# RWKV time mixing on one core: batch 1 in two blocks of 1024 tokens, and the output weight loaded as float32 by the sync queue

## The chip, the core and the metric

The kernel runs on one NeuronCore of a Trainium2 chip. The core has a matrix engine (TensorE, PE in the profile; PEld is its loading of stationary operands), a vector engine (VectorE, DVE), a scalar engine (ScalarE, ACT), a general engine (GpSimd, POOL) and a sync engine (SyncE, SP). Each of them works through its own instructions strictly in the order of the program, and they meet only at semaphores. Transfers are issued by SP, ACT or POOL and carried out by 16 DMA engines, which all queues share. In this kernel POOL issues the transfers that change float32 to bfloat16 on the way (queue q0 in the profile), and SP issues those that only copy (queue q1).

The metric is the device time of one execution, in microseconds (us); lower is better. About 1% (2 us) is what a measurement of this kernel can tell from no change.

## What is computed

```python
batch, seq_len, d_model = (16, 2048, 256)
x_prev[:, 1:, :] = x[:, :-1, :]                      # row 0 is zero
xv = x * time_mix_v + x_prev * (1 - time_mix_v)
xr = x * time_mix_r + x_prev * (1 - time_mix_r)
v = xv.reshape(-1, d_model) @ value_weight
r = xr.reshape(-1, d_model) @ receptance_weight
out = (1 / (1 + exp(-r)) * v) @ output_weight        # float32
```

The reference also computes a key product, which no output depends on.

## The kernel before

The 16 x 2048 tokens are worked in 64 units of 512 tokens (`TU`), four to a batch. For each unit TensorE transposes the tokens so that the 256 features lie on partitions (L272; from batch 10 on the DMA does it), multiplies by the receptance weight into `psum_r` and by the value weight into `psum_v` (both L384, four matmuls of 512 columns), and multiplies the product of the two by the output weight into `psum_o` (L416, eight matmuls of 256 columns, with `wo_bf` as the moving operand). VectorE makes the mixed inputs (scale L354, add L376) and the product `z_sb` of sigmoid and value (L697). ScalarE copies transposes out of PSUM (L289), makes the sigmoids (L658) and copies results out (L471). GpSimd does one half of some scalings (L364) and the small shift copies described next.

**Order on TensorE.** The loop over units `g` (L646) writes the order by hand: the receptance product of unit g, transposes of later units (`advance`, with `START_T = [1, 3, 5, 6, 7, 9, ...]`), the value product of unit g, then the output product of unit g-1. So the first use of `wo_bf` is the output product of unit 0, which stands at the end of loop step 1, behind the value product of unit 1 and ahead of the receptance product of unit 2. The transposes of units 4 and 5, the first two of batch 1, stand in step 2.

**Layout of the tokens.** A transposed unit lies in slots of 128 columns, one slot for each of the j-th tokens of all partitions. The previous token of slot j is slot j-1; the previous token of the first slot is the last slot, one column on. So each separately laid out stretch has one more slot in front, and `wrap_slots` fills it: a copy of 254 elements from the last slot (L557), and a copy of the first column from the stretch before (L554). Batches 0 and 1 (`BYUNIT = 2`) are laid out unit by unit: in DRAM order partition p of a unit holds tokens 4p to 4p+3, so four stretches a batch. Batches from 2 on have one stretch of 2048 tokens. A piece can be scaled only when the last slot of its stretch is transposed.

**Loads at the start.** SP issues units 0 and 1 of batch 0 as float32 (L174, in halves), the receptance weight (L180) and the value weight (L184). GpSimd waits until the receptance weight has landed, and then issues, with the cast to bfloat16: units 2 and 3 of batch 0 (L192), the output weight (L195), and batch 1 as four transfers of one unit (`load(1)`, L152). Batch 2 follows in loop step 1 (`load(2)`, L162), later batches at the places in `LOADS`.

**Stores.** Results of batches 0 and 1 are stored for two units at a time (L474), each partition's rows in two runs of 4 KB.

Of the kernel before, what the change touches and what calls it, by code (L numbers as in the profile page):

```python
# [8 lines left out]
FP32 = mybir.dt.float32  # L9
# [6 lines left out]
def kernel(  # L16
# [25 lines left out]
    nc = tc.nc  # L42

    B, S, D = x.shape
    P = 128
    KO = D // P
    J = S // P
    UJ = 4
    TU = UJ * P
    UB = J // UJ  # L50
    NU = B * UB
    LOOK = 6
    BYUNIT = 2
    LONG = 2
    H = UJ // 2
    STAGED = 10
# [40 lines left out]
    opool = ctx.enter_context(tc.tile_pool(name="opool", bufs=NO))  # L97
# [6 lines left out]
    SYNC = mybir.DependencyInfo(mybir.DependencyClass.Sync, mybir.DependencyReason.DATA)  # L104
# [5 lines left out]
    x_bf = {}  # L110
# [5 lines left out]
    o_sb = {}  # L116
# [12 lines left out]
    def unit_rows(t, b, e, n=1):  # L129

        return t[b, e * TU : (e + n) * TU, :].rearrange("(e p j) d -> p e j d", p=P, j=UJ)

    def new_staged(group):

        x_both[group[0]] = dpool.tile([len(group), PAD + S, D], BF16, name="x_natural")
        for k in range(len(group)):
            x_bf[group[0] + k] = x_both[group[0]][k, PAD:].rearrange("(p j) d -> p j d", p=P)
        return [(group[0], k) for k in range(len(group))]
# [8 lines left out]
    def load(b):  # L147
        if b < STAGED:
            x_bf[b] = xpool.tile([P, J, D], BF16, name="x_bf")
        if b < BYUNIT:  # L150
            for e in range(UB):
                nc.gpsimd.dma_start(  # L152
                    out=x_bf[b][:, e * UJ : (e + 1) * UJ, :], in_=unit_rows(x, b, e)[:, 0]
                )
            return
        if b in HALVED:
            return [
                nc.gpsimd.dma_start(out=x_bf[b][:, j : j + J // 2], in_=rows(b)[:, j : j + J // 2])
                for j in (0, J // 2)
            ]  # L160
        run = 8192 if b < LONG else 16384
        return nc.gpsimd.dma_start(out=x_bf[b], in_=rows(b), max_dma_last_dim=run)  # L162
# [4 lines left out]
    for m, tm in enumerate([time_mix_r, time_mix_v]):  # L167
        nc.scalar.dma_start(
            out=tm_rows[m * KO : (m + 1) * KO, :], in_=tm.rearrange("(ko p) -> ko p", p=P)
        )  # L170

    def load_halves(e):
# [8 lines left out]
        out=w_f32[:, 0], in_=receptance_weight.rearrange("(ko p) n -> p ko n", p=P)  # L181
# [6 lines left out]
    w_prev = consts.tile([P, KO, D], BF16)  # L188
    wo_bf = consts.tile([P, KO, D], BF16)
    x_first = xpool.tile([P, 2, UJ, D], BF16, name="x_bf")  # L190
    for e in (2, 3):
        op = nc.gpsimd.dma_start(out=x_first[:, e - 2], in_=unit_rows(x, 0, e)[:, 0])  # L192
        if e == 2:
            tc.add_manual_dep(op.ins, first_weight.ins.name, SYNC, reason="behind the weight")
    nc.gpsimd.dma_start(out=wo_bf, in_=output_weight.rearrange("(ko p) n -> p ko n", p=P))  # L195
    load(1)

    ones = nc.const_aps.tensor_like(1.0, zeros)
    wide = nc.const_aps.tensor_like(1.0, wo_bf.rearrange("p k d -> p (k d)"))
# [60 lines left out]
    def transposes(i):  # L260

        b, e = divmod(i, UB)
        if b > 0 and e == 0:
            new_xt(b)
        if b >= BYUNIT:
            e = (e - 1) % UB
        j0 = 1 + e * UJ + (e if b < BYUNIT else 0)
        if b < BYUNIT or e == UB - 1:
            late_copies.append((b, e))

        def one(ps, jj, ko, src, idn):
            nc.tensor.transpose(  # L272
                out=ps[:, jj], in_=src[:, jj, ko * P : (ko + 1) * P], identity=idn
            )

        if i == 1:
            for h in (1, 0):
                ps = ps_t_pool.tile([P, H, KO, P], FP32, name="ps_t")
                for jj in range(H):
                    for ko in range(KO):  # L280
                        one(ps[:, :, ko], jj, ko, x_unit[:, i, h * H : (h + 1) * H], ident_f)
                nc.scalar.copy(out=xt[b][:, j0 + h * H : j0 + (h + 1) * H], in_=ps)  # L282
            return
        ps = ps_t_pool.tile([P, UJ, KO, P], BF16, name="ps_t")
        src = x_first[:, e - 2] if b == 0 else x_bf[b][:, e * UJ : (e + 1) * UJ, :]
        for jj in range(UJ):
            for ko in range(KO):
                one(ps[:, :, ko], jj, ko, src, ident)
        nc.scalar.copy(out=xt[b][:, j0 : j0 + UJ], in_=ps)  # L289
        if i in SHIFT_ACT:  # L290
            j, n = (j0 - 1, UJ) if b < BYUNIT else (0, J)
            nc.scalar.copy(out=xt[b][:, j, :, 1:P], in_=xt[b][:, j + n, :, 0 : P - 1])
            shifted.append((b, e))

# [19 lines left out]
    def slots(piece, off=0):  # L314

        b, _, lo, hi = piece
        j = lo // P + (lo // TU if b < BYUNIT else 0) + off
        return slice(j, j + (hi - lo) // P)

    def by_unit(cols, lo, hi):  # L320
# [135 lines left out]
    def output(g, z):  # L456
        b, e = divmod(g, UB)
        if e % 2 == 0:
            new_o(b, e // 2)
        o = o_sb[b, e // 2]  # L460
        j0 = e % 2 * UJ
        if g >= NU - 4:
            for h in range(2):
                ps = ps_t_pool.tile([P, H, D], FP32, name="ps_t")
                out_matmuls(ps, z, b, h * H, H, whole=True)
                nc.scalar.copy(out=o[:, j0 + h * H : j0 + (h + 1) * H, :], in_=ps)
            store(nc.sync, b, e * UJ, (e + 1) * UJ)
            return
        ps = ps_o_pool.tile([P, UJ, D], FP32, name="psum_o")
        out_matmuls(ps, z, b, 0, UJ)  # L470
        nc.scalar.copy(out=o[:, j0 : j0 + UJ, :], in_=ps)  # L471
        if b < BYUNIT:
            if e % 2 == 1:
                nc.sync.dma_start(  # L474
                    out=unit_rows(out, b, e - 1, 2), in_=o.rearrange("p (e j) d -> p e j d", j=UJ)
                )
        elif g >= SINGLE:
            store(nc.sync, b, e * UJ, (e + 1) * UJ)
        elif e % 2 == 1:
            pair = (b, (e - 1) * UJ, (e + 1) * UJ)  # L480
            if g in FIRST:
                firsts.setdefault(FIRST[g], []).append(pair)
            elif g in WAITING:
                kept.setdefault(WAITING[g], []).append(pair)
            else:
                store(nc.sync, *pair)
# [46 lines left out]
    def pieces(g):  # L533

        b, e = divmod(g, UB)
        tile_for(g // 2)
        return [(b, m, e * TU, (e + 1) * TU) for m in range(2)]

    def wrap_slots(piece, one=None, after=None):


        b, _, lo, _ = piece
        by_unit = b < BYUNIT
        key = (b, lo // TU if by_unit else UB - 1)
        if key not in late_copies:
            return
        kos = slice(0, KO) if one is None else slice(one, one + 1)
        if one in (None, KO - 1):
            late_copies.remove(key)
        j = slots(piece).start if by_unit else 0  # L550
        n = UJ if by_unit else J
        if by_unit and j > 0:
            engine = nc.vector if key == (0, 1) else nc.gpsimd
            engine.tensor_copy(out=xt[b][:, j, kos, 0:1], in_=xt[b][:, j - 1, kos, P - 1 : P])  # L554
        if key in shifted:
            return
        op = (nc.vector if after is None else nc.gpsimd).tensor_copy(  # L557
            out=xt[b][:, j, kos, 1:P], in_=xt[b][:, j + n, kos, 0 : P - 1]
        )
        if after is not None:  # L560
            tc.add_manual_dep(op.ins, after.ins.name, SYNC, reason="one at a time")
# [15 lines left out]
    for ko in range(KO):  # L577
        nc.vector.tensor_scalar(
            out=w_prev[:, ko, :],
# [6 lines left out]
        out=w_bf[:, 0, 0, :], in0=w_f32[:, 0, 0, :], scalar1=tms[:, 0, 0:1], scalar2=None, op0=ALU.mult  # L586
    )
    nc.scalar.activation(
        out=w_bf[:, 0, 1, :], in_=w_f32[:, 0, 1, :], func=ACT.Copy, scale=tms[:, 0, 1:2]
# [3 lines left out]
    for ko in range(KO):  # L593
        nc.vector.tensor_scalar(
            out=w_bf[:, 1, ko, :],
# [39 lines left out]
    def scale_act(piece, kos):  # L635
        b, m, _, _ = piece
        for ko in kos:
            nc.scalar.activation(  # L638
                out=mixed(piece, ko),
                in_=tokens(piece, 0, ko),  # L640
                func=ACT.Copy,
                scale=c_sb[:, m, ko : ko + 1],
            )

    z_prev2 = z_prev = None
    for g in range(NU - 1):  # L646
        ps_r = ps_r_pool.tile([P, KO, TU], FP32, name="psum_r")
        if g == 0:
# [5 lines left out]
            last = add(pieces(1)[0])  # L654
# [16 lines left out]
                scale_act(p[0], (0,))  # L671
        for p in [q for q, _ in products[g]] + pooled[g]:
            last_unit_of = p[3] // TU - 1
            need = last_unit_of if p[0] < BYUNIT else min(last_unit_of + 1, UB - 1)
            assert UB * p[0] + need < tnext, (g, p, tnext)
            if g > AHEAD or p not in pooled[g]:
                wrap_slots(p)
        if g == 1:
            load(2)
            scale_act(pieces(2)[1], (1,))  # L680
        for p, kos in products[g]:
            if not (g - 1 >= FREE and p[1] == 1):
# [66 lines left out]
```

## Time and profile before

| | us |
|---|---|
| Time, median of 3 runs | 199.61 |
| The three runs | 199.41, 199.61, 200.61 |
| Span of the profiled execution, first to last instruction | 197.1 |
| Median less span | 2.5 |
| TensorE busy | 191.5 |
| VectorE busy | 183.1 |
| ScalarE busy | 177.1 |
| GpSimd busy | 86.3 |

The profile is one execution; its device time isn't listed by itself beside its span, so the 2.5 us between the span and the median stand here for what lies around the instructions. Times inside the trace count from the first instruction. In the timeline view a row gives the start, the length from the first to the last of the merged instructions, engine, line and operation, and in square brackets the idle time of that engine just before it with what ended it. In the view of the DMAs, a row of an issue gives the size at the destination and the time from the issue to the landing; a row of a queue gives the packets, the bytes at the destination, and the time that its packets took, as a share of 16 engines over the window asked for.

### The profile page before, as it was taken

Reading aid. Unit: us, or ns where it says so; the run is one execution under the profiler, and the core shown is the slowest. Engines: PE = TensorE matmul, PEld = TensorE weight load, DVE = VectorE, ACT = ScalarE, POOL = GpSimd, SP = SyncE. Lnnn points to the kernel's source line nnn. Section 1 sums busy time; section 2 is a strip of 40 time slices with the busy share of each in tenths; the row PEclk is TensorE's granted clock in tenths of the full one; section 3 lists DMA queues with packets and bytes.
Section 4 is the critical chain, followed back from the end, with each engine's and each line's share of the span. In section 5 each row is a group of like instructions: output and inputs, shape, how many; then the busy total and the mean of one; then the engine's idle time right before and its main releaser. Section 6 shows DMA issues by size and latency. Waiting matters only on the chain.

```text
span 197.1 us, 3735 instructions
## 1 busy us (share of the span) xinstructions
PE 191.5 (97%) x1358; PEld 123.0 (62%) x1364; DVE 183.1 (93%) x286; ACT 177.1 (90%) x197; POOL 86.3 (44%) x117
## 2 busy tenths in 40 slices
PE   8999999999999999999999999999999999999992
PEld 3556676666666666666666666666666666666660
DVE  0999999999999999999999999999999999999962
ACT  3699899999999999999999999999999999999982
POOL 2845542443665635624334266444433444444200
PEclk9999999999999999999999999999999999999998
DMA  5999999999999999999999999999999999999985
GB/s 185 238 176 224 218 254 262 247 259 262 296 413 283 283 296 332 283 238 198 376 209 290 335 346 186 212 218 241 290 290 419 419 421 419 416 416 421 382 327 221
DMA packets 35593, 58.13 MB, mean 295 GB/s; under 512 B 26004, under 2 KB 27128, under 8 KB 30840
## 3 DMA queue, kind: packets, MB, share of 16 engines
q1 hardware_dynamic: 31792, 41.34, 60.3%
q0 software_dynamic: 3632, 16.44, 41.6%
q8 instruction: 10, 0.16, 0.3%
q10 hardware_dynamic: 152, 0.13, 0.2%
q14 instruction: 7, 0.06, 0.1%
HBM read 34.34 MB, written 39.90 MB: 377 GB/s over the span
## 4 chain that ended last, share of the span: by engine, by line
PE 90%; DMA 6%; POOL 1%; issue 0%; SPq 0%; ACT 0%
PE psum_r L384 27%; PE psum_v L384 27%; PE psum_o L416 27%; PE ps_t L272 8%; DMA x_bf<-in_x_dram 4%; DMA w_f<-n_receptance_weight_dram 2%; PE ps_t L416 1%; POOL x_bf L192 1%; SPq L174 0%; POOL wo_bf L195 0%; PE psum_v L416 0%; POOL x_bf L152 0%; PE ps_t L384 0%; PE psum_r L416 0%; ACT x_bf L446 0%
## 5 line engine op out<-in xcount | busy, mean ns | idle before, releaser
L364 POOL TENSOR_SCALAR mix<-xt_both,c_sb 128x1024 bf16<-128x1024 bf16 (+1 forms) x55 | 61.1, 1110 | 85.5 <-DVE mix L376 82.3
L697 DVE TENSOR_TENSOR z_sb<-s_sb,psum_v 128x1024 bf16<-128x1024 bf16 (+1 forms) x64 | 76.8, 1201 | 2.3 <-PE psum_v L384 1.1
L376 DVE TENSOR_TENSOR mix<-mix,xt_both 128x1024 bf16<-128x1024 bf16 x112 | 76.8, 696 | 1.4
L384 PEld LDWEIGHTS <-w_bf 128*128 128x128 bf16 x512 | 48.5, 98 | 39.2 <-DVE mix L376 0.8
L658 ACT ACTIVATE s_sb<-psum_r 128x1024 bf16<-128x1024 f32 x63 | 65.2, 1034 | 6.2 <-PE psum_r L384 6.0
L384 PE MATMUL psum_v<-mix,w_bf 128*128 128x512 bf16 (+1 forms) x252 | 64.8, 378 | 0.4 <-DVE mix L376 0.2
L384 PE MATMUL psum_r<-mix,w_bf 128*128 128x512 bf16 x250 | 64.6, 379 | 0.2
L416 PE MATMUL psum_o<-wo_bf,z_sb 128*128 128x256 bf16 x486 | 63.2, 273 | 0.0
L416 PEld LDWEIGHTS <-z_sb 128*128 128x128 bf16 x512 | 52.0, 103 | 17.9 <-DVE z_sb L510 0.7
L471 ACT COPY o_sb<-psum_o 128x1024 f32<-128x1024 f32 x50 | 51.2, 1023 | 5.0 <-PE psum_o L416 4.8
L289 ACT COPY xt_both<-ps_t 128x1024 bf16<-128x1024 bf16 x32 | 32.9, 1039 | 0.0
L272 PEld LDWEIGHTS <-x_bf 128*128 128x128 bf16 x304 | 19.8, 98 | 8.4 <-DMA x_bf<-in_x_dram 0.4
L272 PE MATMUL ps_t<-ident,x_bf 128*128 128x128 bf16 x304 | 22.7, 219 | 0.2 <-DMA x_bf<-in_x_dram 0.2
L354 DVE TENSOR_SCALAR mix<-xt_both,c_sb 128x1024 bf16<-128x1024 bf16 (+1 forms) x47 | 21.3, 463 | 0.0
L638 ACT ACTIVATE mix<-xt_both,c_sb 128x1024 bf16<-128x1024 bf16 x14 | 16.3, 1163 | 0.0
L376 DVE TENSOR_TENSOR mix<-mix,xt_first 128x1024 bf16<-128x1024 bf16 x15 | 10.5, 708 | 0.1
L471 ACT COPY x_bf<-psum_o 128x1024 f32<-128x1024 f32 x10 | 10.2, 1015 | 0.0
L354 DVE TENSOR_SCALAR mix<-xt_first,c_sb 128x512 bf16<-128x512 bf16 x22 | 6.6, 350 | 0.3 <-ACT xt_first L282 0.2
L289 ACT COPY xt_first<-ps_t 128x1024 bf16<-128x1024 bf16 x6 | 6.0, 1022 | 0.0
L557 POOL COPY xt_first<-xt_first 128x254 bf16<-128x254 bf16 x5 | 2.0, 392 | 7.2 <-DVE mix L376 7.2
L162 POOL DMA_DIRECT2D x_bf<-in_x_dram x8 | 4.7, 584 | 0.0
L364 POOL TENSOR_SCALAR mix<-xt_first,c_sb 128x512 bf16<-128x512 bf16 x6 | 4.1, 685 | 1.3 <-DVE mix L376 0.8
(68 smaller groups left out, 52.3 us busy)
## 6 DMA issues: line engine op xcount, KB each, us to landing
out_dram<-o_sb SPq DMA_DIRECT2D x25, 1024.0 KB, 12.1
x_bf<-in_x_dram POOLq DMA_DIRECT2D x8, 1024.0 KB, 15.8
x_natural<-in_x_dram POOLq DMA_DIRECT2D x4, 1024.0 KB, 11.8
out_dram<-x_bf SPq DMA_DIRECT2D x4, 1024.0 KB, 14.4
x_natural<-in_x_dram POOLq DMA_DIRECT2D x4, 512.0 KB, 12.7
out_dram<-x_bf SPq DMA_DIRECT2D x4, 512.0 KB, 4.7
x_bf<-in_x_dram POOLq DMA_DIRECT2D x6, 256.0 KB, 7.0
o_sb<-in_x_dram SPq DMA_DIRECT2D x4, 256.0 KB, 3.9
```

The lines of the kernel that those rows point to most:

```text
L162: return nc.gpsimd.dma_start(out=x_bf[b], in_=rows(b), max_dma_last_dim=run)
L272: nc.tensor.transpose(out=ps[:, jj], in_=src[:, jj, ko * P : (ko + 1) * P], identity=idn)
L289: nc.scalar.copy(out=xt[b][:, j0 : j0 + UJ], in_=ps)
L354: nc.vector.tensor_scalar(out=mixed(piece, ko), in0=tokens(piece, 0, ko), scalar1=c_sb[:, m, ko : ko + 1], scalar2=None, op0=ALU.mult,)
L364: op = nc.gpsimd.tensor_scalar(out=mixed(piece, 1), in0=tokens(piece, 0, 1), scalar1=c_sb[:, m, 1:2], scalar2=1.0, op0=ALU.mult, op1=ALU.mult,
L376: return nc.vector.tensor_tensor(out=mixed(piece), in0=mixed(piece), in1=tokens(piece, 1), op=ALU.add)
L384: nc.tensor.matmul(out=ps[:, mo, :], lhsT=w_bf[:, m, ko, mo * P : (mo + 1) * P], rhs=mixed((b, m, e * TU + lo, e * TU + hi), ko), start=(k ...
L416: nc.tensor.matmul(out=ps[:, j, :], lhsT=slot[:, ko, j], rhs=wo_bf[:, ko, :], start=(ko == 0), stop=(ko == KO - 1),)
L471: nc.scalar.copy(out=o[:, j0 : j0 + UJ, :], in_=ps)
L638: nc.scalar.activation(out=mixed(piece, ko), in_=tokens(piece, 0, ko), func=ACT.Copy, scale=c_sb[:, m, ko : ko + 1],)
L658: nc.scalar.activation(out=s_sb, in_=ps_r, func=ACT.Sigmoid)
L697: nc.vector.tensor_tensor(out=z_sb[:, :, c : c + n], in0=s_sb[:, :, c : c + n], in1=ps_v[:, :, c : c + n], op=ALU.mult,)
```

## The change

Batch 1 gets two stretches of 1024 tokens (`BLOCK = 2 * TU`) in place of four of 512: partition p of a block holds tokens 8p to 8p+7. Its load is two transfers of one block, its results are stored block by block, and its slots, its shift copies and the bookkeeping of what must be transposed first follow the new stretches (`span_of`). Batch 0 stays in units, and batches from 2 on in one stretch. The output weight is no longer cast by a transfer from GpSimd. SP loads it as float32 into a buffer of the pool `o_sb`, and its issue waits for the landing of unit 2; GpSimd casts it to `wo_bf` in loop step 1, right behind the issue of `load(2)`.

```diff
+    BLOCK = 2 * TU
...
+    def block_rows(t, b, h):
+
+        return t[b, h * BLOCK : (h + 1) * BLOCK, :].rearrange("(p j) d -> p j d", p=P)
+
+    def span_of(b):
+
+        return TU if b == 0 else BLOCK if b < BYUNIT else S
...
-        if b < BYUNIT:
-            for e in range(UB):
+        if b == 1:
+            for h in range(S // BLOCK):
                 nc.gpsimd.dma_start(
-                    out=x_bf[b][:, e * UJ : (e + 1) * UJ, :], in_=unit_rows(x, b, e)[:, 0]
+                    out=x_bf[b][:, h * 2 * UJ : (h + 1) * 2 * UJ, :], in_=block_rows(x, b, h)
                 )
             return
...
     x_first = xpool.tile([P, 2, UJ, D], BF16, name="x_bf")
+    wo_f32 = opool.tile([P, KO, D], FP32, name="o_sb")
     for e in (2, 3):
         op = nc.gpsimd.dma_start(out=x_first[:, e - 2], in_=unit_rows(x, 0, e)[:, 0])
         if e == 2:
             tc.add_manual_dep(op.ins, first_weight.ins.name, SYNC, reason="behind the weight")
-    nc.gpsimd.dma_start(out=wo_bf, in_=output_weight.rearrange("(ko p) n -> p ko n", p=P))
+            third = op
     load(1)
+    op = nc.sync.dma_start(out=wo_f32, in_=output_weight.rearrange("(ko p) n -> p ko n", p=P))
+    tc.add_manual_dep(op.ins, third.ins.name, SYNC, reason="behind unit 2")
...
-        j0 = 1 + e * UJ + (e if b < BYUNIT else 0)
-        if b < BYUNIT or e == UB - 1:
+        j0 = 1 + e * UJ + e * TU // span_of(b)
+        if (e + 1) * TU % span_of(b) == 0:
             late_copies.append((b, e))
...
-        if b < BYUNIT:
+        if b == 0:
             if e % 2 == 1:
                 nc.sync.dma_start(
                     out=unit_rows(out, b, e - 1, 2), in_=o.rearrange("p (e j) d -> p e j d", j=UJ)
                 )
+        elif b < BYUNIT:
+            if e % 2 == 1:
+                nc.sync.dma_start(out=block_rows(out, b, e // 2), in_=o)
...
-        by_unit = b < BYUNIT
-        key = (b, lo // TU if by_unit else UB - 1)
+        last = (lo // span_of(b) + 1) * span_of(b) // TU - 1
+        key = (b, last)
...
-        j = slots(piece).start if by_unit else 0
-        n = UJ if by_unit else J
-        if by_unit and j > 0:
+        n = span_of(b) // P
+        j = lo // span_of(b) * (n + 1)
+        if j > 0:
...
         if g == 1:
             load(2)
+            nc.gpsimd.tensor_copy(out=wo_bf, in_=wo_f32)
             scale_act(pieces(2)[1], (1,))
```

The lines left out adapt the indices of slots in the same way.

More of the change, by code (lines that the diff above doesn't have):

```diff
@@ L290, in transposes @@
         if i in SHIFT_ACT:
-            j, n = (j0 - 1, UJ) if b < BYUNIT else (0, J)
+            j, n = 0, J
             nc.scalar.copy(out=xt[b][:, j, :, 1:P], in_=xt[b][:, j + n, :, 0 : P - 1])
@@ L316, in slots @@
         b, _, lo, hi = piece
-        j = lo // P + (lo // TU if b < BYUNIT else 0) + off
+        j = lo // P + lo // span_of(b) + off
         return slice(j, j + (hi - lo) // P)
@@ L673 @@
             last_unit_of = p[3] // TU - 1
-            need = last_unit_of if p[0] < BYUNIT else min(last_unit_of + 1, UB - 1)
+            need = min(last_unit_of + 1, UB - 1)
+            if p[0] < BYUNIT:
+                need = (last_unit_of * TU // span_of(p[0]) + 1) * span_of(p[0]) // TU - 1
             assert UB * p[0] + need < tnext, (g, p, tnext)
```

## The prediction

> **What bounds the kernel now.** I read the page first, then the chain of waits, then the timeline of the first 24 us engine by engine, and last the DMA view in short windows around single issues.
>
> ```profile
> PE 191.5 (97%) x1358; PEld 123.0 (62%) x1364; DVE 183.1 (93%) x286; ACT 177.1 (90%) x197; POOL 86.3 (44%) x117
> ...
> PE   8999999999999999999999999999999999999992
> ...
> PEclk9999999999999999999999999999999999999998
> ...
> PE 90%; DMA 6%; POOL 1%; issue 0%; SPq 0%; ACT 0%
> ```
>
> TensorE is busy 97% of the span at full clock, and the chain that sets the end is TensorE from 15.5 us on. A microsecond in which it stands still is added to the end; a microsecond saved elsewhere is worth nothing unless TensorE waited for it. So the question is what TensorE waits for around the work that the change moves:
>
> ```profile
> 12.11 1.04 PE L384 MATMUL psum_v<-mix,w_bf 128*128 128x512 bf16 x4 [0.25 <-DVE mix L376]
> 12.98 1.04 PE L416 MATMUL psum_o<-wo_bf,z_sb 128*128 128x256 bf16 x8
> 13.86 1.03 PE L384 MATMUL psum_r<-mix,w_bf 128*128 128x512 bf16 x4
> 14.72 0.61 PE L272 MATMUL ps_t<-ident,x_bf 128*128 128x128 bf16 x8
> ...
> 15.54 0.45 PEld L272 LDWEIGHTS <-x_bf 128*128 128x128 bf16 x8 [0.38 <-DMA x_bf<-in_x_dram]
> ...
> 22.25 0.55 PEld L384 LDWEIGHTS <-w_bf 128*128 128x128 bf16 x4 [0.17 <-DVE mix L376]
> ```
>
> The first use of `wo_bf` is at 12.98. Unit 5, the second of batch 1, is waited for 0.38 us at 15.54, and VectorE is waited for 0.17 us at 22.25. Further on its rows carry no bracket until the last unit. These 0.55 us are all that an earlier batch 1 can win, and only the 0.38 us are the DMA's.
>
> ```profile
> 5.58 1.29 POOL L192 DMA_DIRECT2D x_bf<-in_x_dram  x2 [3.90 <-DMA w_f<-n_receptance_weight_dram]
> 6.86 0.74 POOL L195 DMA_DIRECT2D wo_bf<-in_output_weight_dram  x1
> 7.57 2.18 POOL L152 DMA_DIRECT2D x_bf<-in_x_dram  x4
> ...
> 11.29 0.59 POOL L162 DMA_DIRECT2D x_bf<-in_x_dram  x1
> ...
> 13.90 0.39 POOL L557 COPY xt_first<-xt_first 128x254 bf16<-128x254 bf16 x1 [1.80 <-DVE mix L376]
> 14.40 0.68 POOL L364 TENSOR_SCALAR mix<-xt_first,c_sb 128x512 bf16<-128x512 bf16 x1
> ```
> ```profile
> x_bf<-in_x_dram POOLq DMA_DIRECT2D x1, 256.0 KB, 3.8
> wo_bf<-in_output_weight_dram POOLq DMA_DIRECT2D x1, 128.0 KB, 6.0
> w_f<-n_receptance_weight_dram SPq DMA_DIRECT2D x1, 256.0 KB, 3.6
> o_sb<-in_x_dram SPq DMA_DIRECT2D x1, 256.0 KB, 2.8
> ```
>
> Each of these rows is one issue: unit 2 (issued 5.58) lands at 9.4, the output weight (6.86) at 12.9, just ahead of its use at 12.98. The last two are SP's: the receptance weight, issued 1.66, and the first half of unit 0, issued 0.74.
>
> **The change part by part.**
>
> *Removed from GpSimd:* the issue L195 (0.74 us), two of the four issues L152 (2.18/4 = 0.55 each), two shift copies (0.39 each) and some first-column copies. GpSimd is busy 44% and TensorE waits for none of it: worth 0. The batch 1 data leave the queue earlier, since the weight no longer stands ahead of them; worth at most the 0.38 us.
>
> *Blocks:* the same bytes in runs twice as long. Unit 4 now can't be scaled before unit 5 is transposed, but both transposes stand in the same loop step, and the scaling a step later: 0. If that cover went, it would cost one copy of transposes, about 1 us. The stores keep their issues and bytes, one run of 8 KB for two of 4 KB: 0, since no engine waits for a store before its buffer comes round again. Should a load beside one become late, it would be by 8 turns of some 0.17 us more (below), 1.4 us.
>
> *The output weight:* its way becomes unit 2's landing, SP's issue, the transfer beside batch 1, the cast on GpSimd, and only then the matmul at 12.98. TensorE works in order, so the receptance product of unit 2 and all behind it wait with it. Link by link:
>
> Unit 2 lands at 9.4. GpSimd's row at 5.58 came 0.3 us after the landing it waited for (1.66 + 3.6 = 5.26), so SP issues at 9.7. What it costs to get through the DMA engines, no row shows for this transfer; the bounds are these. Alone, 256 KB took SP 2.8 us (landing 12.5). Beside loads from GpSimd, the nearest case is the first store:
>
> ```profile
> 18.97 20.80 SPq L474 DMA_DIRECT2D out_dram<-o_sb  x4
> ...
> q0 software_dynamic: 103, 0.73, 103.9%
> ...
> q1 hardware_dynamic: 15, 0.06, 20.1%
> ```
> ```profile
> q1 hardware_dynamic: 3, 0.01, 80.1%
> ...
> q0 software_dynamic: 24, 0.05, 57.7%
> ...
> q0 software_dynamic: 177, 1.31, 79.7%
> q1 hardware_dynamic: 170, 0.70, 22.7%
> ...
> q0 software_dynamic: 232, 0.42, 112.2%
> ...
> q0 software_dynamic: 175, 0.65, 107.4%
> ```
>
> In the first fence the store is issued at 18.97; the only queue with packets from 19.0 to 22.5 us is q0; its q1 packets begin in the window 22.5 to 23.3, 15 of them, about one on each of the 16 engines. In the second, the first two rows are the windows 1.7 to 1.8 us, where q1's first three packets pass, and 6.9 to 7.5 us, where q0's first 24 do. The next two are one window: from 23 to 31 us, 177 packets of q0 pass and 170 of q1: the engines take one of each in turn, big or small. A packet of q0 took, by share x window x 16 engines over bytes/size: 0.64 us for 8 KB (0.797 x 8 x 16 / 160), 0.18 us for 2 KB (window 13 to 15 us: 1.122 x 2 x 16 / 205) and 0.33 us for 4 KB (window 89.5 to 92.5 us: 1.074 x 3 x 16 / 159). A q1 packet of 4 KB took 0.17 us, so one of 1 KB some 0.05.
>
> The float32 weight is 128 partitions x 2 runs of 1 KB = 256 packets, 16 on each engine. Each must wait its turn behind one packet of q0. Batch 1 in blocks is 4 KB a partition, 8 packets an engine for each block. Units 2 and 3 take 2 x 8 x 0.18 = 2.9 us from about 7.1 us, so the blocks run from about 10.0. The weight's first packet: 9.7, 1.0 us for an issue without company (from 0.74 to the first q1 packets at 1.8), and what stands queued in the engine, 3.5 - 1.0 = 2.5 us for the store, which is four packets of 0.64; here four of 0.18 to 0.33, so 1.0. That gives 11.7. By then 1.7 / 0.33, about 5, of 16 block packets are through. The next 11 turns take 11 x (0.33 + 0.05) = 4.2 us, to 15.9; the last 5 stand beside `load(2)` (issued 11.29, 8 KB packets): 5 x 0.69 = 3.5 us, to 19.4. Landing behind the last packet: 0.6 (unit 2, by the same sum: packets done 8.5, landed 9.4, so 0.9 at most). So 20.0 us, against 12.5 alone. I take the value near the store's row, for that is the same pair of queues.
>
> The cast: 0.3 us for the wake, and for 128x512 on GpSimd 0.68 (L364, the same elements), bounded by
>
> ```profile
> 1.40 0.28 POOL L124 CAST ident<-ident_f 128x128 bf16<-128x128 f32 x1
> ```
>
> at 0.28 to 4 x 0.28 = 1.1. The matmul starts at 21.0: 8.0 us late (5.8 if no packet is queued ahead in the engine, 9 with the slowest DMA engine; minus 0.2 to 1.3 if the weight gets through as if alone). Taken off: the waits that vanish in the stall, 0.38 + 0.17, say 0.6.
>
> Behind the cast on GpSimd stand the shift copy and scaling of unit 3 (13.90 and 14.40) and `load(3)`:
>
> ```profile
> 15.08 0.58 POOL L162 DMA_DIRECT2D x_bf<-in_x_dram  x1
> ...
> x_bf<-in_x_dram POOLq DMA_DIRECT2D x1, 1024.0 KB, 14.9
> ...
> 31.85 0.61 PE L272 MATMUL ps_t<-ident,x_bf 128*128 128x128 bf16 x8
> ```
>
> It lands at 30.0 and is transposed from 31.85. Issued some 1.4 us behind the cast, near 22.5, it goes 7.4 us later, but TensorE comes 9.2 us later too: 0; without the clock's share TensorE comes 7.4 us later, and 1.8 us are still in hand. VectorE needs the copy for unit 3's scaling, some 2.5 us behind the cast in all; TensorE by then has the output product of unit 0, the receptance product and transposes of step 2 to do (0.87 + 0.86 + 0.9 + 0.87): covered, 0; uncovered it would cost 1 us.
>
> *The clock.* A stall of 8 us meets this:
>
> ```profile
> 0.78 2.83 PE L204 MATMUL ps_t<-const-bfloat16-1.0 128*128 128x512 bf16 x7 [0.78 <-PEq L733]
> 3.66 0.98 PE L300 MATMUL psum_r<-ident_f,o_sb 128*128 128x128 f32 x4
> ...
> 192.96 0.39 PE L416 MATMUL psum_o<-wo_bf,z_sb 128*128 128x256 bf16 x2
> ...
> 192.00:195.50 3.50, 1.35 (x9) 0.54 (x8) 1.18 (x3) 1.34 (x3) 0.00 (x0) 1.00 0.85 316
> 195.50:197.00 1.50, 0.00 (x0) 0.00 (x0) 0.00 (x0) 0.00 (x0) 0.00 (x0) 0.52 0.09 29
> ```
>
> At the start the warm-up matmuls of 512 columns come 0.44 us apart (2.83 us for 6.25 of them), against 0.22 in the row at 12.11 (0.87 to the next group, for four). At the end the granted clock (the column behind POOL's) halves 2.2 us after the last matmul (193.3 to 195.5). So the clock halves in the stall, and TensorE restarts cold; by the start, for 2.8 to 4 us, take 3.6, of which half is lost: 1.8 us.
> By the Trainium skill (TensorE: Matmul & The Clock Gate, Part 1: The HAM clock gate) the clock is gated by a free-running window of about 3.4 us that must be idle, or busy, as a whole; by that the sum is an estimated 1.7 to 3.4 us here and zero for stalls below 3.4 us; the 2.2 us at the end agree only if the few last matmuls count as idle.
>
> *Sum:* 8.0 - 0.6 + 1.8 = 9.2 us. Span 197.1 + 9.2 = 206.3; with the 2.5 us between this span and the median of 199.61, 208.8 us.
>
> **The rivals.**
>
> 1. *The weight gets through, no change.* If an engine passes the weight's 16 small packets together rather than one a turn, the last goes 0.8 + 0.3 us behind the first: 10.7 to 11.7 becomes 11.8 to 12.8, landing 12.3 to 13.3, matmul at 13.3 to 14.3, 0.3 to 1.3 us late; less 0.6, -0.3 to +0.7: 199.3 to 200.3, middle 199.8. For it: the store's packets are 4 KB, the weight's 1 KB, and no row shows small packets of q1 beside q0. Against it: the 177 to 170. It decides from about 4 packets a turn. What the change says of batch 1 is then true and worth 0.4 at most.
> The Trainium skill (DMA: Bandwidth & Descriptors, Queues, rings and completion order) speaks for this rival: an engine takes the queues in turn, but drains a whole packet, typically 9 to 17 descriptors, before it switches. Our rows count one for one, but with runs of 4 KB, so no run here tests it for 1 KB.
>
> 2. *Late, but the clock holds.* Eager stationary loads or a stall near 6 us leave the clock up: 208.8 - 1.8 = 207.0, with the short stall 199.6 + 5.8 - 0.6 = 204.8. For it: the start shows only the cold side of the gate. Against it: 2.2 us sufficed at the end.
>
> 3. *Faster by more than 1%.* 2 us would have to be won where TensorE waits 0.55 us in all behind 12.98. Nothing in the profile has that size.
>
> **How the numbers follow.** The forecast with late weight and lost clock gets 0.60, rival 2 0.14, rival 1 0.23, rival 3 0.03. The likeliest's own range is 205 to 211.5 (stall 5.8 to 9, clock 1.4 to 3.4, less 0.6). Without rival 1 more than 2 in 10 would be left out, so the range goes from 199.4 to 211.5. About 1%, 2 us, is what can be told from no change: slower 0.60 + 0.14 = 0.74, within 0.23, faster 0.03.
>
> **What would show it.** Right: TensorE idle for 6 to 9 us ahead of the first L416, released by GpSimd's cast; the cast's own wait ended by a DMA that took 8 to 11 us; a lower PEclk in slices 2 to 5; q0 and q1 packets alternating from 12 to 19 us. Wrong: the weight landing within 4 us of its issue, and L416 near 13.5. Unit 5's wait at 15.54 should be gone either way.

## The result, and the profile after

The changed kernel takes 211.71 us (median of 6 runs, 211.49 to 212.53) against 199.51 us for the kernel before in the same comparison: 12.2 us slower by the medians; the ratio of the runs is 1.0629, 95% interval 1.0599 to 1.066. The forecast was 208.8 us and a range to 211.5 us: the sign, the place and the chain of causes held, and the size was 2.9 us short, just outside the range. The profiled execution took 212.4 us with a span of 210.6 us, 13.5 us longer than the span of before; the spans of the other five were 209.7 to 210.7 us. In every execution on record with a span, the time is about 1.8 us longer than the span; so only 1.8 of the 2.5 us between the span of before and its median lie around the instructions, and the span of 197.1 us belongs to about 198.9 us. The profiled execution of before was thus 0.6 us shorter than the median of 199.51, and that of after 0.7 us longer than its own: these 1.3 us are the difference between 13.5 and 12.2. In all comparisons an execution over 1.5% longer than the fastest of its kernel is left out of the ratio.

The page of the changed kernel, busy time per engine and the first rows by slices (a slice is 5.3 us):

```profile
PE 194.6 (92%) x1358; PEld 124.7 (59%) x1364; DVE 183.6 (87%) x286; ACT 177.4 (84%) x197; POOL 83.3 (40%) x111
...
PE   8940499999999999999999999999999999999992
...
PEclk9995579999999999999999999999999999999999
```

Counted from 1, TensorE has a hole in slices 3 to 5 that it did not have, and a lower clock in slices 4 to 6, within the hole and right behind it. The rest of the row is full as before. Its busy time has grown by 3.1 us for the same 1358 instructions; most of that is the slow clock (below). The hole in the timeline, engine by engine in order of time:

```profile
9.90 0.38 SPq L207 DMA_DIRECT2D o_sb<-in_output_weight_dram  x1
...
11.23 0.59 POOL L171 DMA_DIRECT2D x_bf<-in_x_dram  x1
...
12.05 1.04 PE L396 MATMUL psum_v<-mix,w_bf 128*128 128x512 bf16 x4 [0.19 <-DVE mix L388]
...
23.20 0.61 POOL L697 CAST wo_bf<-o_sb 128x512 bf16<-128x512 f32 x1 [11.38 <-DMA o_sb<-in_output_weight_dram]
...
23.86 1.86 PE L428 MATMUL psum_o<-wo_bf,z_sb 128*128 128x256 bf16 x8 [10.76 <-POOL wo_bf L697]
...
25.52 1.91 PE L396 MATMUL psum_r<-mix,w_bf 128*128 128x512 bf16 x4
27.22 1.91 PE L284 MATMUL ps_t<-ident,x_bf 128*128 128x128 bf16 x16
28.93 1.26 PE L396 MATMUL psum_v<-mix,w_bf 128*128 128x512 bf16 x4
30.03 1.04 PE L428 MATMUL psum_o<-wo_bf,z_sb 128*128 128x256 bf16 x8
```

Read from the matmul at 23.86 backwards: TensorE was idle for 10.76 us, released by GpSimd's cast; the cast's engine was idle for 11.38 us, released by the transfer of the output weight; that transfer had been issued at 9.90. The same matmul began at 12.98 before, so it is 10.9 us late. Behind it, four matmuls of 512 columns take 1.7 us from group to group (25.52 to 27.22) where they took 0.87.

How the weight passed, in the DMA view of the changed kernel: the queues from 10.9 to 13.3 us (one row), from 13.4 to 16.4 us and from 16.9 to 21.0 us (two rows each; packets, MB at the destination, share of 16 engines).

```profile
q0 software_dynamic: 119, 0.45, 99.2%
...
q0 software_dynamic: 139, 0.55, 94.2%
q1 hardware_dynamic: 119, 0.12, 14.3%
...
q0 software_dynamic: 102, 0.80, 93.4%
q1 hardware_dynamic: 106, 0.11, 9.5%
```

In the first window SP's queue moves nothing, though the transfer was issued at 9.90. In the second its packets pass one for one with the packets of GpSimd's queue: 119 beside 139, of which 13 are under 512 B, 9 are of 8 KB and the other 117 are the 4 KB packets of batch 1's second block. That is 119 in 3.0 us on 16 engines, so one turn in 0.40 us. In the third they pass one for one with the 8 KB packets of batch 2, one turn in 0.62 us (4.1 x 16 / 106). On average seven of each engine's 16 packets go in the second window, seven in the third. The queue's last two packets pass between 22.6 and 22.9 us, so the weight has landed by about 22.9, and the cast starts at 23.20.

And the clock, by stretches of the stall and behind it (windows view of the changed kernel; the figure behind POOL's is the granted clock):

```profile
13.10:15.70 2.60, 0.00 (x0) 0.00 (x0) 2.35 (x4) 1.00 (x2) 0.00 (x0) 1.00 0.99 201
15.80:23.80 8.00, 0.00 (x0) 0.00 (x0) 0.00 (x0) 0.00 (x0) 0.60 (x2) 0.50 0.76 163
23.90:29.30 5.40, 5.40 (x29) 3.53 (x29) 1.97 (x4) 2.85 (x4) 1.78 (x5) 0.50 0.54 86
29.40:33.00 3.60, 3.60 (x28) 2.29 (x27) 2.70 (x6) 2.81 (x4) 1.62 (x3) 1.00 0.97 178
```

TensorE works at half clock from 23.86 to 29.4, 5.5 us, and loses half of that, about 2.75 us.

So the profiled execution adds up: stall 10.9, clock 2.75, less the waits of before that vanished in the stall (0.38 for unit 5 and 0.17 for VectorE, 0.6 as forecast) is 13.05 us. The output product of unit 3 (timeline of before, then of after) starts at 36.18 where it started at 23.13, 13.05 us later:

```profile
23.13 0.49 PE L416 MATMUL psum_o<-wo_bf,z_sb 128*128 128x256 bf16 x3
```
```profile
36.18 1.04 PE L428 MATMUL psum_o<-wo_bf,z_sb 128*128 128x256 bf16 x8
```

The remaining 0.45 us of the span come in small steps, 0.17 us between units 3 and 6 and 0.29 us at units 45 and 46. The steps at units 45 and 46 stand in the traces of e1 and e3 too, so they are not the late weight's; they are not explained here.

### The profile page after: what moved, and what is told of

It is laid out like the page before. It is cut to its first block, busy times and chain, and to the rows that moved or that the text cites. A ratio compares the mean times of both kernels' runs of the same rounds, so it can differ in the third digit from the quotient of the medians.

```text
span 210.6 us, 3730 instructions
## 1 busy us (share of the span) xinstructions
PE 194.6 (92%) x1358; PEld 124.7 (59%) x1364; DVE 183.6 (87%) x286; ACT 177.4 (84%) x197; POOL 83.3 (40%) x111
## 4 chain that ended last, share of the span: by engine, by line
PE 83%; issue 7%; DVE 5%; ACT 2%; POOL 1%; POOLq 0%; ACTq 0%
PE psum_r L396 24%; PE psum_o L428 24%; PE psum_v L396 23%; PE ps_t L284 7%; DVE z_sb L715 2%; DVE mix L388 2%; PE ps_t L216 1%; DVE mix L366 1%; PE ps_t L428 1%; ACT xt_first L294 1%; PE psum_r L312 1%; ACT s_sb L673 1%; ACT o_sb L483 0%; PE psum_r L410 0%; ACT xt_both L301 0%
## 5 line engine op out<-in xcount | busy, mean ns | idle before, releaser
L428 PE MATMUL psum_o<-wo_bf,z_sb 128*128 128x256 bf16 x486 | 64.0, 275 | 10.8 <-POOL wo_bf L697 10.8
L483 ACT COPY o_sb<-psum_o 128x1024 f32<-128x1024 f32 x50 | 51.1, 1021 | 17.3 <-PE psum_o L428 16.9
L396 PE MATMUL psum_r<-mix,w_bf 128*128 128x512 bf16 x250 | 65.4, 383 | 0.2
L284 PEld LDWEIGHTS <-x_bf 128*128 128x128 bf16 x304 | 20.5, 100 | 8.7 <-DMA x_bf<-in_x_dram 0.8
L284 PE MATMUL ps_t<-ident,x_bf 128*128 128x128 bf16 x304 | 23.4, 224 | 0.0
L697 POOL CAST wo_bf<-o_sb 128x512 bf16<-128x512 f32 x1 | 0.6, 606 | 11.4 <-DMA o_sb<-in_output_weight_dram 11.4
## 6 DMA issues: line engine op xcount, KB each, us to landing
out_dram<-x_bf SPq DMA_DIRECT2D x4, 1024.0 KB, 13.8
```

Of the source, the lines that this page charges most:

```text
L284: nc.tensor.transpose(out=ps[:, jj], in_=src[:, jj, ko * P : (ko + 1) * P], identity=idn)
L396: nc.tensor.matmul(out=ps[:, mo, :], lhsT=w_bf[:, m, ko, mo * P : (mo + 1) * P], rhs=mixed((b, m, e * TU + lo, e * TU + hi), ko), start=(k ...
L428: nc.tensor.matmul(out=ps[:, j, :], lhsT=slot[:, ko, j], rhs=wo_bf[:, ko, :], start=(ko == 0), stop=(ko == KO - 1),)
```

## Experiments

The theory: the weight's packets, on SP's queue, get one turn for each packet of GpSimd's queue, and only after a wait; the late weight and the clock it costs are the whole loss. The rivals: batch 1's blocks cost something too; a float32 weight by SP is slow as such; the queues share by bytes or time, not by turns; the clock is hidden behind other engines. Each run is compared with the kernel before on the same chip.

**e1: the blocks without the weight.**

```diff
-    wo_f32 = opool.tile([P, KO, D], FP32, name="o_sb")
...
+    nc.gpsimd.dma_start(out=wo_bf, in_=output_weight.rearrange("(ko p) n -> p ko n", p=P))
     load(1)
-    op = nc.sync.dma_start(out=wo_f32, in_=output_weight.rearrange("(ko p) n -> p ko n", p=P))
-    tc.add_manual_dep(op.ins, third.ins.name, SYNC, reason="behind unit 2")
...
-            nc.gpsimd.tensor_copy(out=wo_bf, in_=wo_f32)
```

> Batch 1 stays in blocks; the output weight goes back to GpSimd's casting transfer at its old place. Theory (the late weight is the whole loss): no stall ahead of the first output product, full clock, 199.5 us within 0.6. Rival (the blocks cost something too, by the wait of unit 4 for unit 5 or by larger packets): above 201 us.

Measured: 199.72 us against 199.34 us, ratio 1.0027, interval 0.9993 to 1.006. The first output product, in this run's timeline, waits for nothing:

```profile
13.75 1.04 PE L426 MATMUL psum_o<-wo_bf,z_sb 128*128 128x256 bf16 x8
```

No difference that can be told. By themselves the blocks cost nothing that can be told, and win nothing; the rival is out. Whether they matter beside a late weight is a question for e2.

**e2: the weight without the blocks.** To the kernel before (`load(1)` in four units):

```diff
+    wo_f32 = opool.tile([P, KO, D], FP32, name="o_sb")
...
-    nc.gpsimd.dma_start(out=wo_bf, in_=output_weight.rearrange("(ko p) n -> p ko n", p=P))
+            third = op
     load(1)
+    op = nc.sync.dma_start(out=wo_f32, in_=output_weight.rearrange("(ko p) n -> p ko n", p=P))
+    tc.add_manual_dep(op.ins, third.ins.name, SYNC, reason="behind unit 2")
...
             load(2)
+            nc.gpsimd.tensor_copy(out=wo_bf, in_=wo_f32)
```

> Batch 1 in four units as before; the weight as float32 by SP behind unit 2. The packets of GpSimd's queue are 2 KB instead of 4 KB. If what stands ahead of SP's first packet is an amount of data or time (about 2.4 us, as in the changed kernel and at the first store of before): first packet near 13.3 us, 13 turns of 0.24 us and 3 of 0.68, landing near 19.2, first output product near 20.1, 208.6 us. If it is a count of packets (four): first packet near 11.6, landing near 16.2, 205 us. If SP's packets wait until the transfer in progress on GpSimd's queue is done: first packet near 11.4, about the same 205 us.

Measured: 206.76, 207.49 and 208.47 us, and 210.84 us in the profiled execution, which is left out of the ratio: 1.0395, interval 1.0316 to 1.0474, so 207.2 us beside the 199.34 us of before. The weight alone costs about 8 us, two thirds of the loss of 12.2 us. As the blocks alone cost nothing (e1), the other 4 us arise only where both meet. The turns explain the direction: one turn beside a 2 KB packet takes 0.21 us (2.0 x 16 / 151, from the rows below), beside a 4 KB packet 0.40 us, so with blocks fewer of the weight's packets are through when the 8 KB packets of batch 2 come. Because the profiled execution was the longest of the four (span 209.0 us against 205.0 to 206.7), only its DMA rows are used here: the issue, the queues from 11.0 to 13.75 us (one row), and from 13.8 to 15.8 us (two rows).

```profile
10.25 0.38 SPq L198 DMA_DIRECT2D o_sb<-in_output_weight_dram  x1
...
q0 software_dynamic: 301, 0.55, 110.0%
...
q0 software_dynamic: 167, 0.31, 81.8%
q1 hardware_dynamic: 151, 0.15, 27.0%
```

Nothing of SP's passes up to 13.75, 3.5 us behind the issue, and then its packets go one for one with the 2 KB packets (0.31 MB are 151 of them). A count of four packets ahead would have put the start at 11.6, and a wait for the end of the transfer in progress at 11.4; an amount of time or data put it at 13.3, and that is what came, plus the 0.5 us by which the issue was late. The first output product starts at 22.41 in this long execution, 2.3 us later than expected.

**e3: the weight by SP at once.**

```diff
     op = nc.sync.dma_start(out=wo_f32, in_=output_weight.rearrange("(ko p) n -> p ko n", p=P))
-    tc.add_manual_dep(op.ins, third.ins.name, SYNC, reason="behind unit 2")
```

> The changed kernel without SP's wait for unit 2: the weight is issued at 3.6 us, behind the value weight. Theory (it is late because it queues among GpSimd's packets): it passes before they come, lands near 8.5 us, no stall, unit 5 is not waited for; 199.2 us, between 198.9 and 199.8. Rival (a float32 weight by SP and the cast are slow as such): above 203 us.

Measured: 200.51 us against 199.34 us, ratio 1.005, interval 1.0015 to 1.0086. One wait less takes away 11 of 12 us: a float32 weight by SP and a cast on GpSimd are not slow as such. But the gain that was expected did not come: 200.51 lies outside 198.9 to 199.8, and the run is slower than before by about 0.5%, less than the 1% that a measurement of this kernel was taken to tell. The timeline of this run (the issue, TensorE's transposes of unit 2, its first use of the weight), and unit 2's landing in the DMA view:

```profile
3.61 0.47 SPq L207 DMA_DIRECT2D o_sb<-in_output_weight_dram  x1
...
11.12 0.45 PEld L283 LDWEIGHTS <-x_bf 128*128 128x128 bf16 x8 [1.70 <-DMA x_bf<-in_x_dram]
...
13.76 1.04 PE L427 MATMUL psum_o<-wo_bf,z_sb 128*128 128x256 bf16 x8
```
```profile
x_bf<-in_x_dram POOLq DMA_DIRECT2D x1, 256.0 KB, 5.2
```

The weight now goes ahead of unit 2, which lands 5.2 us behind its issue instead of 3.8, and TensorE's weight loads wait 1.70 us for it. The first output product starts 0.8 us later than before. Later TensorE waits twice for VectorE, 0.29 us at 21.88 and 0.25 us at 23.61. That the weight's new place ahead of unit 2 makes the 0.5% is not shown: this is one profiled execution, no run tried to shift unit 2, and in e1's profiled execution the first output product also starts at 13.75, since there the receptance weight landed late and unit 2 was issued only at 6.68.

**e5: the weight in half as many packets.**

```diff
-    op = nc.sync.dma_start(out=wo_f32, in_=output_weight.rearrange("(ko p) n -> p ko n", p=P))
+    op = nc.sync.dma_start(out=wo_f32, in_=output_weight.rearrange("(p ko) n -> p ko n", p=P))
```

> The changed kernel with the output weight read in one run of 2 KB a partition instead of two of 1 KB, so 8 packets an engine instead of 16 for the same bytes (the rows of the output weight come to other partitions, so the result is that of a permuted weight). If the engines take one packet of each queue in turn: first packet near 13.4 us, 8 turns of 0.43 us beside the second block, landing near 17.3, first output product near 18.2; stall 5.2 us and 1.7 to 2.8 us of clock: 206.4 us, between 205.5 and 207.3. If the queues share the engines by bytes or time: no change, 211.7 us.

Measured: 206.80 us, ratio 1.0378, interval 1.0343 to 1.0413. Issue and first use in the timeline, and the queues from 13.4 to 16.4 us:

```profile
9.93 0.33 SPq L207 DMA_DIRECT2D o_sb<-in_output_weight_dram  x1
...
18.66 1.86 PE L428 MATMUL psum_o<-wo_bf,z_sb 128*128 128x256 bf16 x8 [5.54 <-POOL wo_bf L697]
```
```profile
q0 software_dynamic: 126, 0.50, 83.7%
q1 hardware_dynamic: 120, 0.24, 23.3%
```

The same 256 KB in 128 packets instead of 256: again about one for one (the rows count 12 packets under 512 B too), nearly all of the 128 gone by 16.4, and the stall is 5.54 us instead of 10.76. In this kernel the engines share by turns, not by bytes. Sharing by bytes or time would have left 211.7.

**e6: batch 2's load behind the cast.**

```diff
-            load(2)
             nc.gpsimd.tensor_copy(out=wo_bf, in_=wo_f32)
+            load(2)
```

> The changed kernel with the cast ahead of the issue of batch 2's load on GpSimd, so that no 8 KB packet of batch 2 is in GpSimd's queue while the weight passes. In turns: first packet near 13.4, 8 turns beside the second block, then 8 packets without company; landing near 17.2, first output product near 18.1, 206 us, between 205 and 207; batch 2 then lands about 26 us and is not waited for. Rival (SP's packets are slow by themselves, whatever stands beside them): 211 us or more.

Measured: 206.64 us, ratio 1.0371, interval 1.0332 to 1.041.

```profile
19.09 1.86 PE L428 MATMUL psum_o<-wo_bf,z_sb 128*128 128x256 bf16 x8 [5.92 <-POOL wo_bf L696]
```

The weight still has 256 packets, but behind the second block nothing stands beside them, and the stall is 5.92 us. So batch 2's 8 KB packets made nearly half of the changed kernel's stall. The matmul was expected at 18.1 and came at 19.1: the first packet passed at 13.7 instead of 13.4, and the last between 18.0 and 18.1, where the landing was expected at 17.2; the cast began at 18.43.

**e4 and e7: TensorE kept busy in the stall**, with 44 and with 38 matmuls of 512 columns on constants ahead of the first output product.

```diff
+        if g == 1:
+            warm_up(176)
         if z_prev is not None and not LATE_O <= g < NU - 3:
             output(g - 1, z_prev)
```

(e7 has 152 in place of 176.)

> The changed kernel with 44 additional matmuls of 512 columns on constants ahead of the first output product, which fill 9.5 us of TensorE's stall and are used by nothing. Theory (the lost clock is a term of its own): clock 1.00 throughout, the stall ends at the same place, 2.2 to 2.8 us less than the changed kernel, about 209.1 us. Rival (VectorE and ScalarE set the pace behind the stall, so that the clock is hidden): 211.7 us.

> As the run with 44 additional matmuls, with 38 (8.2 us), so that they end well before the weight is cast. That run gave 210.6 us, 1.1 less than the changed kernel, where its trace shows the clock at 1.00 and 2.7 us won in step 2. If the additional matmuls themselves ended too late: 209.2 us here. If something else takes back what the clock wins: 210.6 us again, and the trace is to show a later end of the stall.

Measured: e4 210.62 us, ratio 1.0544, interval 1.0468 to 1.0619; e7 211.16 us, ratio 1.0614, interval 1.0543 to 1.0686. Neither expectation of e7 holds: not 209.2, and the stall ends where it did. The intervals can't tell e7 from the changed kernel; the traces can. Its windows (the additional matmuls, the rest of the stall, the 5.4 us behind it) and the rows of its timeline in steps 2 to 4:

```profile
13.10:21.40 8.30, 8.30 (x39) 3.68 (x37) 2.41 (x4) 1.05 (x2) 0.00 (x0) 1.00 1.06 225
21.50:23.90 2.40, 0.00 (x0) 0.00 (x0) 0.00 (x0) 0.00 (x0) 0.62 (x2) 1.00 0.14 27
23.90:29.30 5.40, 5.36 (x47) 3.76 (x47) 3.57 (x6) 4.29 (x5) 2.34 (x6) 1.00 0.54 77
```
```profile
23.94 1.03 PE L428 MATMUL psum_o<-wo_bf,z_sb 128*128 128x256 bf16 x8 [2.48 <-POOL wo_bf L697]
...
27.43 1.04 PE L428 MATMUL psum_o<-wo_bf,z_sb 128*128 128x256 bf16 x8
...
31.78 1.04 PE L396 MATMUL psum_r<-mix,w_bf 128*128 128x512 bf16 x4 [0.27 <-DVE mix L388]
...
33.51 1.04 PE L396 MATMUL psum_v<-mix,w_bf 128*128 128x512 bf16 x4 [0.25 <-DVE mix L388]
...
34.39 1.04 PE L428 MATMUL psum_o<-wo_bf,z_sb 128*128 128x256 bf16 x8
```

The clock stays at 1.00, and the output product of unit 1 starts at 27.43 instead of 30.03, 2.6 us earlier. Then TensorE waits for VectorE, which the slow TensorE of the changed kernel did not do in these steps, and by the output product of unit 3 only 1.8 us are left (34.39 against 36.18). So in these two traces the clock is worth 2.6 us where it is lost and 1.8 us behind VectorE, and the two spans (208.8 and 210.6 us) differ by 1.8 us as well. In the medians it shows as less: e4 is 11.3 us and e7 11.9 us above before, the changed kernel 12.2 us, and the intervals overlap.

## Why the prediction came out as it did

The chain of the forecast was right link by link: the wait for unit 2, the packets one for one beside batch 1 and then batch 2, the cast, the matmul in order on TensorE, the clock. What was wrong is the size of two terms of the sum. In the profiled executions it came to 13.5 us where 9.2 were forecast: 2.9 us of the difference are the stall (10.9 for 8.0), 0.95 the clock (2.75 for 1.8), 0.45 the small steps. The stall is the landing of the weight: 20.0 us forecast, about 22.9 measured.

- **What stands queued ahead in the engine** was put at four packets, 1.0 us for packets of 0.18 to 0.33 us. It is not a count of packets. With 8 KB packets the first packet came 3.5 us behind the issue (before), with 4 KB 3.45 us (after: issued 9.90, none up to 13.35), with 2 KB 3.55 us (e2). So 2.4 us should have stood where 1.0 stood, and the first packet at 13.35 instead of 11.7. This is the step that failed: the store's row gave 2.5 us, and I scaled it by packet size without a row that showed the scaling.
- **The turns** themselves were sized well: 0.40 and 0.62 us measured, 0.38 and 0.69 forecast. But the later start left 8 of them for batch 1's block and 8 for batch 2 in place of 11 and 5, so the first error grew by 0.5 us (8.2 for 7.7).
- **SP's issue** came at 9.90 instead of 9.7, since unit 2 landed half a microsecond later in this execution: small.
- **The end of the transfer.** These three make 2.1 us of the 2.9. From 13.35, 8 turns of each kind end at 21.55; the last packets passed between 22.6 and 22.9, where the forecast took 0.6 us from the last packet to the landing. The 16 engines end apart: 14 packets pass from 21.5 to 22.0 us, five from 22.0 to 22.9. The forecast knew such a spread ("9 with the slowest DMA engine") but kept it out of its sum.
- **The cast**: 0.61 us measured, 0.68 forecast. **The wait for the shift copy behind it** was covered, as said.
- **The clock**: 1.8 us was forecast, half of a cold stretch of 3.6 us taken from the start. The stretch was 5.5 us, and 2.75 us were lost in it. That e7 leaves 1.8 us behind VectorE is luck: the forecast's 1.8 counts no VectorE. Of the 0.6 us of vanished waits the changed kernel shows all: in its steps 2 to 4 TensorE waits for nothing.
- **Rival 1** (the weight gets through) is refuted, and with it the rule that was quoted for it, in this kernel: by the Trainium skill (DMA: Bandwidth & Descriptors, Queues, rings and completion order) an engine drains a packet of typically 9 to 17 descriptors before it switches queues; the runs of 1 KB passed one a turn (119 beside 126 of 4 and 8 KB; 106 beside 98 of 8 KB, counted by bytes), and e5's runs of 2 KB too. **Rival 2** (the clock holds) is refuted by the granted clock of 0.50. **Rival 3** had no size, and no run gained anything: e1's trace still waits 0.27 us for batch 1 at 15.92, and e3, which no longer waits for it there, is not faster.
- Two of the signs lay outside their own bounds: TensorE was idle for 10.76 us (6 to 9 forecast), and the weight took 13.0 us from issue to landing (8 to 11).
- The upper end of the range, 211.5, was built from a stall of at most 9 us. A bound of 2.5 us ahead in the engine, which the nearest row gave unscaled, belonged into it: 1.5 us more there, and with the turns that this moves to batch 2 it would have held 211.7. (The lower end of the likeliest's own range is 206.2 by its terms, 199.6 + 5.8 + 1.4 - 0.6, and not 205.)

No version tried is faster than the kernel before. e1 can't be told from it, and e3 is 0.5% slower.

## What to carry to other kernels

A transfer on one queue beside a busy other queue is priced in turns, not in bytes: count its packets on each engine, and multiply by the duration of the packets that it will meet, including those of loads issued after it. In this kernel fewer, longer runs helped as much as an empty queue (e5 against e6), and longer packets on the other queue, which cost nothing alone (e1), made the competing transfer later (e2 against the changed kernel). Before moving a small transfer from a queue where it stands in order to one where it competes, ask which instruction first needs it, and how far behind the issue its first packet can come; here issuing it before the other queue filled (e3) was worth 11 us.

## What the runs showed that had not been expected

**The first packet's delay does not depend on the size of the packets it meets.** 1.05 us without company, and about 3.5 us beside a full queue of 8 KB, 4 KB or 2 KB packets. It is not always 3.5 us: in e5 and e7 SP's first store was issued (25.81 and 29.71) when GpSimd's queue had only about 30 and 65 packets of 8 KB left, two and four an engine, and its first packet came when nearly all of these were through, 0.9 and 2.6 us behind the issue. All of these packets move about the same bytes in a time, so the runs do not tell whether the 3.5 us beside a full queue are an amount of data or a time; that stays open.

**The clock's switching depends on more than the length of the pause.** Windows of e5, in which TensorE stopped at the same place (13.1) and started at 18.66:

```profile
13.10:18.10 5.00, 0.03 (x1) 0.00 (x0) 2.39 (x4) 1.04 (x2) 0.09 (x1) 1.00 1.08 240
18.20:21.50 3.30, 2.83 (x11) 1.58 (x11) 1.97 (x4) 0.94 (x1) 2.30 (x6) 0.50 1.18 221
```

Here the clock held for 5.0 us of idleness, then fell, and was back 2.9 us after the restart; in the changed kernel it fell after 2.6 us and took 5.5 us. From the fall to the return it is 3.4 us here (18.2 to 21.6), 13.65 us in the changed kernel (15.75 to 29.4) and 6.8 us in e6 (18.0 to 24.8): one, four and two times 3.4 us. By the Trainium skill (TensorE: Matmul & The Clock Gate, Part 1: The HAM clock gate) the gate looks at a free-running window of about 3.4 us; the runs agree with that, since these stretches are whole multiples of it and the same pause meets the window at different places. They do not agree with a window that must be idle as a whole, as the forecast read it: 2.6 us of idleness, less than a window, made the clock fall in the changed kernel. So the price of a stall depends on where it meets the window, and can change from run to run: the mean granted clock is 0.966 to 0.967 in two of the changed kernel's six executions and 0.971 to 0.972 in the other four, whose spans are 0.7 to 1.0 us shorter.
